# A second feed-forward's gate and up products: one group of seven over 1024 rows in place of two over 512

## The chip, the core and the metric

The kernel runs on one core of a Trainium2 chip. The core has five engines, each with its own instruction queue: TensorE multiplies, VectorE and ScalarE work element by element, GpSimd and SyncE are used here almost only to issue transfers. SBUF is the working memory with 128 partitions; PSUM holds TensorE's results, in eight banks of 128 x 512 float32 values.

The metric is the device time of one execution, in microseconds. The kernel before takes 1819.21 us (median of three runs, 1818.37 to 1819.67).

## What is computed

The reference is one layer of a streaming encoder on 256 rows of 2048 values: a half feed-forward, a mixer (a state-space group and an attention group between an input and an output projection), a second half feed-forward, and a gated embedding. The change touches the second feed-forward alone:

```python
def swiglu(h, w_gate, w_up, w_down):
    return (jax.nn.silu(h @ w_gate) * (h @ w_up)) @ w_down

x = x + 0.5 * swiglu(rms_norm(x, ffn2_norm[i]), ffn2_w_gate[i], ffn2_w_up[i], ffn2_w_down[i])
```

`h` is 256 x 2048, `w_gate` and `w_up` are 2048 x 5632, `w_down` is 5632 x 2048, all in float32.

## The kernel before

**Precision.** Every float32 operand is split into a high part (`hi`, a cast on ScalarE) and a low part (`lo`, a subtraction on VectorE; both in `split`, lines 178 to 187). A product is three matmuls: high by high, low by high, high by low. One matmul takes 128 rows of the contraction, 128 tokens and 512 columns.

**Blocks.** Gate and up are computed in 11 blocks of 512 columns (`f` = 0 to 10, the loop in `ffn`, line 633), gate and up of a block together. The 2048 rows of the contraction are four quarters of 512 (`kb` = 0 to 3); a quarter of one weight for one block is a load of 1 MB, into one of five `raw` buffers. A quarter is two halves; a half (128 x 1024 values) is split into a pair `hi`, `lo`. Pairs come from seven buffers in turn (`weight_pair`, line 288: four `whi`/`wlo`, three `shi`/`slo`; before the first chunk only the four).

**Columns.** `Seven.column` (line 591) multiplies a quarter in the plain way: per half 12 matmuls, 6 for each of the two token tiles.

**Chunks: seven products in place of eight.** `Seven.chunk` (line 566) treats a quarter of both weights as a 2 x 2 by 2 x 2 block product by the scheme of Strassen and Winograd: left blocks are two halves of the contraction by two token tiles, right blocks are `b11`, `b21` (gate) and `b12`, `b22` (up). It takes seven products of 6 matmuls, 42 in place of 48. For that VectorE forms three sums of weights (`t1`, `t2`, `t4`), GpSimd adds a fourth by an accumulating transfer (`b12 += b22`), and the sums of activations are formed once, by `whole_rows` and `sum_forms`. The products go into seven PSUM banks (1 to 7, and 8 for columns); `opened`, `gated` and `ended` (lines 647 to 688) put them together: one ScalarE copy, four 512-wide and two 1024-wide additions on VectorE, two SiLU on ScalarE, and the multiplication of gate and up. `turned` then transposes the block on VectorE, and SyncE moves its quarters into place (`turn_quarters`).

**The second feed-forward.** Block 0 multiplies quarter 1 by columns, quarter 0 by a chunk, quarters 2 and 3 by columns, and forms the activation sums of quarters 0 and 1 on the way. Blocks 1 to 10 each do: chunk of quarter 0, gate columns of quarters 2 and 3, chunk of quarter 1, up columns of quarters 2 and 3.

**What sets the order.** Each engine's instructions run in one fixed order that is planned when the kernel is built. TensorE's and SyncE's are close to the order of the code; VectorE's and ScalarE's are mixed from several products. An instruction waits for the data and the buffers it needs. `put_off(n, ...)` places work n steps later; a step is two products in a chunk or one column half.

Of the kernel before, what the change touches and what calls it, by code (L numbers as in the profile page):

```python
# [9 lines left out]
F32 = mybir.dt.float32  # L10
# [23 lines left out]
def layer_kernel(ctx: ExitStack, tc: tile.TileContext, a: dict, shapes: dict, out: bass.AP):  # L34
# [38 lines left out]
    def phase(name):  # L73
        return tc.tile_pool(name=name, bufs=1, reuse_waits="tile")
# [103 lines left out]
    def split(hi, lo, src, scale=None, pinned=False):  # L178

        if scale is None:  # L180
            copy = nc.scalar.copy(hi, src)  # L181
            if pinned:
                pin(copy)
            rest = nc.vector.tensor_tensor(out=lo, in0=src, in1=hi.bitcast(F32), op=ALU.subtract)  # L184
# [130 lines left out]
        nc.sync.dma_start(raw[:, :nk, :], quarter(w, k0 // 4, n0))  # L315
        return weight_split(raw, nk, own)

    def gemm_half(ps, half, ts, start, stop, cols=slice(0, NB)):

        (ahi, alo), (h, hi, lo) = half  # L320
        for j in range(2):
            for t in ts:
                lh = ahi[:, 2 * h + j, t * P : (t + 1) * P]
                ll = alo[:, 2 * h + j, t * P : (t + 1) * P]
                nc.tensor.matmul(ps[t], lhsT=lh, rhs=hi[:, j, cols], start=start and j == 0, stop=False)  # L325
                nc.tensor.matmul(ps[t], lhsT=ll, rhs=hi[:, j, cols], start=False, stop=False)  # L326
        for j in range(2):
            for t in ts:
                lh = ahi[:, 2 * h + j, t * P : (t + 1) * P]
                nc.tensor.matmul(ps[t], lhsT=lh, rhs=lo[:, j, cols], start=False, stop=stop and j == 1)  # L330

    def gemm_block(act, w, n0, nkt, first=()):

# [108 lines left out]
    def whole_rows(pool, parts, pinned=False):  # L442

        hi, lo = parts
        u = pool.tile([P, 2, NB], F32, tag="sum", name=uid("whole"), bufs=2)
        added = nc.vector.tensor_tensor(
            out=u.rearrange("p j n -> p (j n)"), in0=hi.bitcast(F32).rearrange("p j t -> p (j t)"),
            in1=lo.bitcast(F32).rearrange("p j t -> p (j t)"), op=ALU.add,
        )
# [4 lines left out]
    def sum_forms(pool, u, kind="n"):  # L454
# [4 lines left out]
        for z, (x, y, op) in enumerate((  # L459
            (a21, a22, ALU.subtract), (s[:, 0], a11, ALU.subtract),  # L460
            (a11, a21, ALU.subtract), (a12, s[:, 1], ALU.add),
        )):
            nc.vector.tensor_tensor(out=s[:, z], in0=x, in1=y, op=op)
        both = halves(kind)
        split(*both, sums.rearrange("p j n -> p (j n)").rearrange("p (z t) -> p z t", z=4))
        return both

# [135 lines left out]

    shared = (1, 5, 6, 7)

    def ffn(i, xn, nxt, bg=None):
        wg, wu, wd = (a[f"ffn{i}_w_{s}"] for s in ("gate", "up", "down"))
        hT = []
# [7 lines left out]
        turns = sevens  # L616
        sums = []
        mids = {}

        def turned(hp, f, hh):  # L620
            pair, n_pair = f // 2, min(2, NF - f // 2 * 2) * 4
# [11 lines left out]
        for f in range(NF):  # L633
            for kb, (at, steps) in enumerate(((2, 8), (5, 11))):
                if bg and f == at:
                    put_off(steps, lambda kb: sums.append(sum_forms(sevens, whole_rows(sevens, xn(kb), pinned=True), "h")), kb)
            if prep and f == early:
                finish(prep)
                side.close()
                prep = None  # L640
                turns = pools.enter_context(phase(f"turns{i}"))
                hp = pools.enter_context(phase(f"h{i}b"))
            if f >= early or f in alone:
                sg, hh = com("sg"), com("h")
                gate_cols, up_cols = ([u[:, t * NB : (t + 1) * NB] for t in range(TT)] for u in (sg, hh))

                def opened(s, g=gate_cols, u=up_cols):
                    nc.scalar.copy(g[0], s.bank(1))
                    nc.vector.tensor_tensor(out=u[0], in0=s.bank(6), in1=g[0], op=ALU.add)
                    nc.vector.tensor_tensor(out=u[1], in0=s.bank(7), in1=u[0], op=ALU.add)  # L650

                def gated(s, g=gate_cols, u=up_cols, hh=hh):
                    for z, (ps, other) in enumerate(((s.bank(2), g[0]), (s.bank(4), u[1]))):
                        nc.vector.tensor_tensor(out=g[z], in0=ps, in1=other, op=ALU.add)
                        nc.scalar.activation(g[z], g[z], AF.Silu, scale=xn.rs(z))
# [5 lines left out]
                s = Seven(xn, lambda kb: sums[kb], ((wg, f * NB), (wu, f * NB)), sevens, turns)  # L661
                if f == 0:
                    sums.append(sum_forms(sevens, whole_rows(sevens, xn(0))))
                    s.column(0, (1,))
                    s.column(1, (1,))
                    s.chunk(0, shared)
                    put_off(0, opened, s)
                    s.column(0, (2,))
                    s.column(1, (2,))
                    s.column(0, (3,), True)  # L670
                    sums.append(sum_forms(sevens, whole_rows(sevens, xn(1))))
                elif f in alone:
                    s.single(0, gate_cols[0], *up_cols)
                    s.column(0, (1, 2, 3), True)
                else:
                    s.chunk(0)
                    s.column(0, (2, 3))
                    s.chunk(1, (*shared, 2, 4))
                    put_off(0, opened, s)
                put_off(0, gated, s)  # L680

                def ended(s, g=gate_cols, u=up_cols, hh=hh, f=f, hp=hp):
                    nc.vector.tensor_tensor(out=hh, in0=s.banks[3.8], in1=hh, op=ALU.add)
                    for t in range(TT):
                        nc.vector.scalar_tensor_tensor(
                            out=u[t], in0=u[t], scalar=xn.rs(t), in1=g[t], op0=ALU.mult, op1=ALU.mult
                        )
# [36 lines left out]
            put_off(2, turned, hp, f, hh)  # L724
# [1074 lines left out]
```

## Time and profile before

| | |
|---|---|
| median of three runs | 1819.21 us |
| the profiled execution, its own time | 1818.46 us |
| its span, first to last instruction | 1816.4 us |
| mean granted TensorE clock | 0.999 |
| second feed-forward, gate and up (blocks 0 to 10) | about 1028 to 1480 us of the span |

The profile is one execution, taken by the hardware profiler. Its page gives the busy time of each engine: PE is TensorE, DVE is VectorE, ACT is ScalarE, POOL is GpSimd, SP is SyncE. Its views used below are the waits (which engine waited for which, us in total, how often, the longest), the busy time in stretches, the groups of like instructions (line, engine, operation, output<-input, shapes, count; busy us, mean ns of one; idle time before them and what ended it), the timeline (start, duration, engine, line, operation) and the issues of transfers (KB each, median us to landing). An instruction's duration in the timeline overlaps the next one's, so that the spacing of starts says what one costs.

### The profile page before, as it was taken

Reading aid. Unit: us, or ns where it says so; the run is one execution under the profiler, and the core shown is the slowest. Engines: PE = TensorE matmul, PEld = TensorE weight load, DVE = VectorE, ACT = ScalarE, POOL = GpSimd, SP = SyncE. Lnnn points to the kernel's source line nnn. Section 1 sums busy time; section 2 is a strip of 40 time slices with the busy share of each in tenths; the row PEclk is TensorE's granted clock in tenths of the full one; section 3 lists DMA queues with packets and bytes.
Section 4 is the critical chain, followed back from the end, with each engine's and each line's share of the span. In section 5 each row is a group of like instructions: output and inputs, shape, how many; then the busy total and the mean of one; then the engine's idle time right before and its main releaser. Section 6 shows DMA issues by size and latency. Waiting matters only on the chain.

```text
span 1816.4 us, 24219 instructions
## 1 busy us (share of the span) xinstructions
PE 1806.7 (99%) x8918; PEld 1496.6 (82%) x8918; DVE 1573.9 (87%) x1839; ACT 1065.3 (59%) x1240; POOL 106.2 (6%) x162
## 2 busy tenths in 40 slices
PE   9999999999999999999999999999999999999998
PEld 7888888888888888888898888888888888888887
DVE  8978889999998896697567899999999999889775
ACT  7445455656565665455695566555565566567664
POOL 0020100000000001110021000000000010000000
PEclk9999999999999999999999999999999999999999
DMA  8799867777776667674636787787767787666563
GB/s 321 268 292 301 269 221 232 235 259 228 262 261 226 190 226 262 188 255 163 218 139 215 234 297 225 263 268 235 232 231 236 241 277 242 220 209 228 195 243 128
DMA packets 107655, 428.41 MB, mean 236 GB/s; under 512 B 24368, under 2 KB 48336, under 8 KB 65136
## 3 DMA queue, kind: packets, MB, share of 16 engines
q1 hardware_dynamic: 96256, 390.06, 60.8%
q0 software_dynamic: 10560, 35.40, 9.0%
q8 instruction: 70, 1.15, 0.2%
q10 hardware_dynamic: 720, 1.41, 0.2%
q14 instruction: 49, 0.40, 0.1%
HBM read 372.41 MB, written 10.88 MB: 211 GB/s over the span
## 4 chain that ended last, share of the span: by engine, by line
PE 96%; DVE 1%; DMA 1%; issue 1%; ACT 1%; SPq 0%; DVEq 0%; ACTq 0%
PE acc L325 16%; PE acc L326 16%; PE acc L330 16%; PE aux L330 7%; PE aux L326 7%; PE aux L325 7%; PE acc L509 5%; PE acc L506 5%; PE acc L507 5%; PE aux L509 3%; PE aux L506 3%; PE aux L507 3%; DMA raw<-in_ffn_w_gate 0%; PE aux L1210 0%; PE acc L1466 0%
## 5 line engine op out<-in xcount | busy, mean ns | idle before, releaser
L184 DVE TENSOR_TENSOR wlo<-raw,whi 128x1024 fp32r<-128x1024 f32 x480 | 580.7, 1222 | 123.5 <-ACT whi L181 120.5
L181 ACT CAST whi<-raw 128x1024 fp32r<-128x1024 f32 x480 | 498.2, 1050 | 291.9 <-PE acc L326 181.8
L325 PE MATMUL acc<-whi,nhi 128*128 128x512 f32 x908 | 356.3, 392 | 2.8 <-ACT whi L277 2.3
L326 PE MATMUL acc<-whi,nlo 128*128 128x512 f32 x908 | 353.7, 390 | 0.0
L330 PE MATMUL acc<-wlo,nhi 128*128 128x512 f32 x908 | 252.5, 389 | 0.0
L184 DVE TENSOR_TENSOR slo<-raw,shi 128x1024 fp32r<-128x1024 f32 x186 | 226.1, 1216 | 15.8 <-ACT shi L181 15.5
L181 ACT CAST shi<-raw 128x1024 fp32r<-128x1024 f32 x186 | 195.2, 1049 | 62.1 <-DMA raw<-in_ffn_w_down 20.3
L325 PEld LDWEIGHTS acc<-whi,nhi 128*128 128x128 f32 x908 | 170.4, 188 | 40.3 <-ACT whi L277 3.5
L330 PEld LDWEIGHTS acc<-wlo,nhi 128*128 128x128 f32 x908 | 170.3, 188 | 35.9 <-DVE wlo L184 0.3
L326 PEld LDWEIGHTS acc<-whi,nlo 128*128 128x128 f32 x908 | 170.5, 188 | 34.8 <-DVE nlo L278 0.3
L181 ACT CAST whi<-sum 128x1024 fp32r<-128x1024 f32 x79 | 83.3, 1054 | 159.6 <-DVE sum L513 141.5
L181 ACT CAST shi<-sum 128x1024 fp32r<-128x1024 f32 x59 | 62.1, 1053 | 104.0 <-DVE sum L513 90.8
L513 DVE TENSOR_TENSOR sum<-sum,raw 128x1024 f32<-128x1024 f32 x92 | 112.1, 1219 | 1.0
L184 DVE TENSOR_TENSOR wlo<-sum,whi 128x1024 fp32r<-128x1024 f32 x79 | 96.2, 1220 | 7.3 <-ACT whi L181 6.7
L574 POOL DMA_DIRECT2D raw<-raw x44 | 38.2, 867 | 1035.7 <-DVE sum L513 595.0
L325 PE MATMUL aux<-whi,nhi 128*128 128x512 f32 x220 | 85.6, 389 | 0.0
L326 PE MATMUL aux<-whi,nlo 128*128 128x512 f32 x220 | 85.6, 389 | 0.0
L184 DVE TENSOR_TENSOR slo<-sum,shi 128x1024 fp32r<-128x1024 f32 x59 | 72.0, 1220 | 1.2 <-ACT shi L181 0.5
L330 PE MATMUL aux<-wlo,nhi 128*128 128x512 f32 x220 | 67.7, 389 | 0.0
L325 PE MATMUL acc<-whi,hhi 128*128 128x512 f32 x156 | 60.7, 389 | 0.0
L326 PE MATMUL acc<-whi,hlo 128*128 128x512 f32 x156 | 60.7, 389 | 0.0
L513 DVE TENSOR_TENSOR sum<-raw,raw 128x1024 f32<-128x1024 f32 x46 | 56.0, 1217 | 5.1 <-DMA raw<-in_ffn_w_down 4.2
(390 smaller groups left out, 3404.1 us busy)
## 6 DMA issues: line engine op xcount, KB each, us to landing
raw<-in_ffn_w_up SPq DMA_DIRECT2D x88, 1024.0 KB, 5.8
raw<-in_ffn_w_down SPq DMA_DIRECT2D x88, 1024.0 KB, 4.9
raw<-in_ffn_w_gate SPq DMA_DIRECT2D x86, 1024.0 KB, 6.9
raw<-in_w_in SPq DMA_DIRECT2D x32, 1024.0 KB, 5.5
raw<-raw POOLq DMA_DIRECT2D x46, 512.0 KB, 5.6
raw<-in_w_out SPq DMA_DIRECT2D x16, 1024.0 KB, 4.9
raw<-in_w_ple_gate SPq DMA_DIRECT2D x16, 1024.0 KB, 5.5
hT<-mid SPq DMA_DIRECT2D x160, 64.0 KB, 4.8
```

What stands on the lines that cost most here:

```text
L181: copy = nc.scalar.copy(hi, src)
L184: rest = nc.vector.tensor_tensor(out=lo, in0=src, in1=hi.bitcast(F32), op=ALU.subtract)
L325: nc.tensor.matmul(ps[t], lhsT=lh, rhs=hi[:, j, cols], start=start and j == 0, stop=False)
L326: nc.tensor.matmul(ps[t], lhsT=ll, rhs=hi[:, j, cols], start=False, stop=False)
L330: nc.tensor.matmul(ps[t], lhsT=lh, rhs=lo[:, j, cols], start=False, stop=stop and j == 1)
L506: nc.tensor.matmul(ps, lhsT=lh[j], rhs=hi[:, j], start=begin and j == 0, stop=False)
L507: nc.tensor.matmul(ps, lhsT=ll[j], rhs=hi[:, j], start=False, stop=False)
L509: nc.tensor.matmul(ps, lhsT=lh[j], rhs=lo[:, j], start=False, stop=z in final and j == 1)
L513: nc.vector.tensor_tensor(out=t, in0=x, in1=y, op=ALU.add)
L574: nc.gpsimd.dma_start(b12, b22, accum_op=ALU.add)
```

## The change

Blocks 1 to 10 of the second feed-forward no longer use two chunks of 512 rows. A new class `Wide` does one group of seven over 1024 rows: quarter 0 of gate and up are `b11` and `b12`, quarter 1 are `b21` and `b22`, and each of the seven products now has 12 matmuls (two halves). The running sums that `opened` and `gated` formed on VectorE stay in PSUM: between products ScalarE copies one bank into another with the sign turned (`handed`), and the next product is added on top of it. A block so needs five banks; `b5` is copied out once by ScalarE.

In five blocks (2, 4, 6, 8, 9) a third group, of quarter 2, is joined: each of the seven products gets one more half (18 matmuls), and the columns are then only those of quarter 3. The other five blocks keep columns of quarters 2 and 3, after the seven products.

Block 0 is reordered: columns of quarters 0 and 1, a chunk of quarter 2 (with sign-turned sums, kept in buffers of their own, `third`), then the activation forms of quarters 0 and 1 together (`wide_forms`), then columns of quarter 3. The first feed-forward is unchanged.

The core of the diff:

```diff
+    def wide_forms(pool, parts, kind="n"):
+
+        u0, u1 = (whole_rows(pool, p) for p in parts)
+        (a11, a21), (a12, a22) = ([u[:, :, 4 * t : 4 * t + 4] for t in range(TT)] for u in (u0, u1))
+        for o, x, y in ((a22, a21, a22), (a21, a11, a21), (a11, a11, a22), (a12, a12, a11)):
+            nc.vector.tensor_tensor(out=o, in0=x, in1=y, op=ALU.subtract)
+        forms = []
+        for u in (u0, u1):
+            both = halves(kind)
+            split(*(in_32(v) for v in both), u)
+            forms.append(both)
+        return forms
...
+        def multiply(self, ps, z, parts, fresh=False):
+            left = self.left(z)
+            for i, ((lh, ll), (hi, lo)) in enumerate(zip(left, parts)):
+                for j in range(2):
+                    nc.tensor.matmul(
+                        ps, lhsT=lh[j], rhs=hi[:, j], start=fresh and i == 0 and j == 0, stop=False,
+                        skip_group_check=True,
+                    )
+                    nc.tensor.matmul(ps, lhsT=ll[j], rhs=hi[:, j], start=False, stop=False, skip_group_check=True)
+                for j in range(2):
+                    nc.tensor.matmul(
+                        ps, lhsT=lh[j], rhs=lo[:, j], start=False, stop=i == len(left) - 1 and j == 1,
+                        skip_group_check=True,
+                    )
+            step()
+
+        def handed(self, out, ps):
+            nc.scalar.activation(out, ps, AF.Copy, scale=-1.0)
+
+        def seven(self):
+
+            if ring[0] is None:
+                ring[:] = [self.turns, 0]
+            b11, b12 = self.load(0, 0), self.load(1, 0)
+            if self.third:
+                ga, ua_ = self.load(0, 2), self.load(1, 2)
+                b11, b12 = b11 + ga[:1], b12 + ua_[:1]
+            b22, b21 = self.load(1, 1), self.load(0, 1)
+            t = [self.pool.tile([P, 2, NB], F32, tag="sum", name=uid("sum"), bufs=2) for _ in range(2)]
+            if self.third:
+                b22, b21 = b22 + ua_[1:], b21 + ga[1:]
+                t.append(self.third[1].tile([P, 2, NB], F32, tag="sum3", name=uid("sum3")))
+
+            def add(x, y):
+                for o, u, v in zip(t, x, y):
+                    nc.vector.tensor_tensor(out=o, in0=u, in1=v, op=ALU.add)
+
+            b2, b5 = acc(), acc()
+            p = self.prepare(b11)
+            self.multiply(b2, "11", p, True)
+            add(b11, b12)
+            for u, v in zip(b12, b22):
+                nc.gpsimd.dma_start(u, v, accum_op=ALU.add)
+            p = self.prepare(t)
+            self.multiply(b5, 0, p, True)
+            double = aux()
+            b3, b8 = double[:, :NB], double[:, NB:]
+            add(t, b22)
+            p = self.prepare(t)
+            self.handed(b3, b2)
+            self.multiply(b3, 1, p)
+            p = self.prepare(b21)
+            self.multiply(b2, "12", p)
+            b4 = acc()
+            p = self.prepare(b12)
+            self.handed(b4, b3)
+            self.multiply(b4, 2, p)
+            add(t, b21)
+            p = self.prepare(b22)
+            self.multiply(b3, 3, p)
+            p = self.prepare(t)
+            self.handed(b8, b4)
+            self.multiply(b4, "22", p)
...
+            if not bg and f:
+                joined = f in (2, 4, 6, 8, 9)
+                s = Wide(
+                    xn, sums, ((wg, f * NB), (wu, f * NB)), sevens, turns, (third, narrow) if joined else None
+                )
+                s.seven()
+                sg, hh, five = com("sg"), com("h"), com("sq")
+                put_off(0, nc.scalar.copy, five, s.five)
+                kbs = (3,) if joined else (2, 3)
+                s.column(0, kbs)
...
+                put_off(0, gate)
+                s.column(1, kbs)
+                nc.vector.tensor_tensor(
+                    out=hh.rearrange("p (t n) -> p t n", t=TT), in0=s.double.rearrange("p (t n) -> p t n", t=TT),
+                    in1=five.unsqueeze(1).to_broadcast([P, TT, NB]), op=ALU.add,
+                )
+                for t in range(TT):
+                    cols = slice(t * NB, (t + 1) * NB)
+                    nc.vector.scalar_tensor_tensor(
+                        out=hh[:, cols], in0=hh[:, cols], scalar=xn.rs(t), in1=sg[:, cols], op0=ALU.mult, op1=ALU.mult
+                    )
...
                 if f == 0:
-                    sums.append(sum_forms(sevens, whole_rows(sevens, xn(0))))
+                    s.column(0, (0,))
+                    s.column(1, (0,))
                     s.column(0, (1,))
+                    sum_forms(sevens, whole_rows(sevens, xn(2)), both=third, turned=True)
                     s.column(1, (1,))
-                    s.chunk(0, shared)
+                    s.chunk(2, shared)
                     put_off(0, opened, s)
-                    s.column(0, (2,))
-                    s.column(1, (2,))
+                    sums = wide_forms(sevens, [xn(0), xn(1)])
                     s.column(0, (3,), True)
-                    sums.append(sum_forms(sevens, whole_rows(sevens, xn(1))))
```

`prepare` loads nothing: it splits the two or three halves that it is given into pairs. A step is now one product of the seven, or one column half.

More of the change, by code (lines that the diff above doesn't have):

```diff
@@ L316, in weight_halves, with gemm_half @@
         return weight_split(raw, nk, own)
-    def gemm_half(ps, half, ts, start, stop, cols=slice(0, NB)):
+    def gemm_half(ps, half, ts, start, stop, cols=slice(0, NB), joined=False):
         (ahi, alo), (h, hi, lo) = half
@@ L324, in gemm_half @@
                 ll = alo[:, 2 * h + j, t * P : (t + 1) * P]
-                nc.tensor.matmul(ps[t], lhsT=lh, rhs=hi[:, j, cols], start=start and j == 0, stop=False)
-                nc.tensor.matmul(ps[t], lhsT=ll, rhs=hi[:, j, cols], start=False, stop=False)
+                nc.tensor.matmul(
+                    ps[t], lhsT=lh, rhs=hi[:, j, cols], start=start and j == 0, stop=False, skip_group_check=joined
+                )
+                nc.tensor.matmul(
+                    ps[t], lhsT=ll, rhs=hi[:, j, cols], start=False, stop=False, skip_group_check=joined
+                )
         for j in range(2):
@@ L329, in gemm_half @@
                 lh = ahi[:, 2 * h + j, t * P : (t + 1) * P]
-                nc.tensor.matmul(ps[t], lhsT=lh, rhs=lo[:, j, cols], start=False, stop=stop and j == 1)
+                nc.tensor.matmul(
+                    ps[t], lhsT=lh, rhs=lo[:, j, cols], start=False, stop=stop and j == 1, skip_group_check=joined
+                )
     def gemm_block(act, w, n0, nkt, first=()):
@@ L452, in whole_rows, with sum_forms @@
         return u.rearrange("p j n -> p (j n)").rearrange("p (j x b) -> p j x b", j=4, b=32)
-    def sum_forms(pool, u, kind="n"):
+    def sum_forms(pool, u, kind="n", both=None, turned=False):
         sums = pool.tile([P, 2, NB], F32, tag="sum", name=uid("rows"), bufs=2)
@@ L618, in ffn @@
         mids = {}
+        if not bg:
+            side = pools.enter_context(ExitStack())
+            narrow = side.enter_context(phase(f"third{i}"))
+            third = [narrow.tile([P, 4, T], F32R, name=uid("third")) for _ in range(2)]
         def turned(hp, f, hh):
@@ L648, in opened @@
                     nc.scalar.copy(g[0], s.bank(1))
-                    nc.vector.tensor_tensor(out=u[0], in0=s.bank(6), in1=g[0], op=ALU.add)
+                    nc.vector.tensor_tensor(
+                        out=u[0], in0=g[0], in1=s.bank(6), op=ALU.add if bg else ALU.subtract
+                    )
                     nc.vector.tensor_tensor(out=u[1], in0=s.bank(7), in1=u[0], op=ALU.add)
```

63 lines of the change are left out of this document (59 added, 4 removed).

## The prediction

> **What bounds the kernel now.** I read the page first, then TensorE's waits and the busy time by block in the stage that is changed, and then the timelines of TensorE, VectorE and SyncE there. The page's first lines:
>
> ```profile
> span 1816.4 us, 24219 instructions
> PE 1806.7 (99%) x8918; PEld 1496.6 (82%) x8918; DVE 1573.9 (87%) x1839; ACT 1065.3 (59%) x1240; POOL 106.2 (6%) x162
> ```
>
> TensorE looks full. Whether it is bound by itself is read from its waits between 940 and 1500 us, of which there is one, and from the blocks (columns: stretch, length, then busy us of PE, PEld, DVE, ACT, POOL with their instructions, clock, DMA share, GB/s):
>
> ```profile
> PE acc L509 <- DVE slo L184: 0.4, 1, 0.4
> ```
>
> ```profile
> 1030.00:1071.90 41.90, 41.46 (x183) 34.02 (x182) 41.67 (x56) 27.39 (x35) 2.30 (x3) 1.00 0.79 277
> 1071.90:1112.70 40.80, 40.80 (x182) 33.78 (x181) 40.06 (x40) 25.15 (x28) 1.74 (x2) 1.00 0.70 232
> 1112.70:1153.50 40.80, 40.80 (x182) 33.78 (x181) 38.54 (x38) 22.20 (x24) 1.71 (x2) 1.00 0.79 258
> ...
> 1439.40:1480.60 41.20, 41.20 (x183) 34.12 (x182) 40.13 (x43) 25.12 (x27) 5.28 (x9) 1.00 0.84 272
> ```
>
> The rows are blocks f=0, 1, 2 and 10. Three rows of TensorE's timeline give the price of a matmul: f=0 starts, its chunk starts 48 matmuls later, f=1 starts.
>
> ```profile
> 1027.96 0.39 PE L325 MATMUL acc<-whi,hhi 128*128 128x512 f32 x1
> ...
> 1038.85 0.39 PE L506 MATMUL acc<-whi,hhi 128*128 128x512 f32 x1
> ...
> 1070.86 0.39 PE L506 MATMUL acc<-shi,hhi 128*128 128x512 f32 x1
> ```
>
> 10.89 us / 48 = 0.2269 us a matmul. A block after f=0 has 180 (two chunks of 42, eight column halves of 12): 40.84 us, the length of its row. So TensorE sets the pace, with nothing between matmuls; f=0 has 186, 42.2 us, and took 42.9. But VectorE is busy for 38.5 to 41.7 us of the same rows: it is the engine that is late next. Its real price is the spacing of starts (VectorE's timeline, block f=10):
>
> ```profile
> 1431.15 0.68 DVE L654 TENSOR_TENSOR sg<-acc,sg 128x512 f32<-128x512 f32 x1
> 1431.75 0.68 DVE L654 TENSOR_TENSOR sg<-acc,h 128x512 f32<-128x512 f32 x1
> ...
> 1441.65 1.41 DVE L685 SCALAR_TENSOR_TENSOR h<-h,sm,sg 128x512 f32<-128x512 f32 x2
> 1442.97 1.30 DVE L217 STREAM_TRANSPOSE mid<-h 128x512 f32<-128x512 f32 x2
> 1444.19 1.18 DVE L184 TENSOR_TENSOR wlo<-raw,whi 128x1024 fp32r<-128x1024 f32 x1
> ...
> 1446.43 1.22 DVE L184 TENSOR_TENSOR wlo<-raw,whi 128x1024 fp32r<-128x1024 f32 x1
> ...
> 1457.78 1.22 DVE L184 TENSOR_TENSOR wlo<-raw,whi 128x1024 fp32r<-128x1024 f32 x1
> ```
>
> Between the last two are nine more of the same width: 11.35 us for ten, 1.135 each ("a wide op" below). A 512-wide one takes 0.60, the two gatings 1.32, the two transposes 1.22. A block before: 28 wide ops (14 splits and 6 sums in chunks, 8 column splits) 31.8; four 512-wide and one wide in opened and gated 3.5; wide, gatings, transposes at the end ("the tail") 3.7; together 39.0 of 40.8.
>
> **The change: what TensorE saves.** Two groups of seven over 512 rows are 84 matmuls, one group over 1024 rows is 84 too. Only the third group saves: 7 x 18 + 48 = 174 instead of 180, in five blocks: 30 matmuls, 6.8 us. That is the ceiling of the gain.
>
> **What VectorE does per block.** opened and gated go (-3.5), the tail stays. A block without the third group ("plain"): 28 wide + 3.7 = 35.5 of 40.8. One with it ("joined"): 21 + 4 splits, 9 sums, 34 wide = 38.6 + 3.7 = 42.3 against TensorE's 39.5. A pair: 77.8 against 80.3. The average fits, but only with work done ahead.
>
> **How far ahead it must be.** The seven products come first now, P1 to P7, and the column halves, cheap for VectorE (1.135 per 2.72 us of TensorE), last. In a plain block the first half of P6 is VectorE's 17th wide op: 19.3 us, with the last block's tail 23.0. TensorE gets there after 5 x 2.72 = 13.6 us and wants the low part 4 matmuls (0.9) later. So VectorE must stand 8.5 us ahead when P1 starts. Joined: 25th op, 28.4 + 3.7 - 5 x 4.08 - 0.9 = 10.8. The seven pairs of split buffers allow, at P1, six pairs and the sums between: 10 ops (11.4 us) in a plain block, 12 (13.6) in a joined one. Enough, where the block before had plain columns (21.8 us of TensorE for 9.1). A joined block uses up 34.1 + 3.7 - 28.6 = 9.2 of it, and its columns return 10.9 - 4.5 = 6.4: f=8 starts with 13.6, f=9 with 10.8 against a need of 10.8, f=10 with 8.0 against 8.5. Cost there: 0.5 us (0 to 3, since a lost DMA or cast shows at once).
>
> **What f=0 does to that lead.** Here I choose the sign. VectorE from f=0's start to f=1's:
>
> ```profile
> 1027.27 1.22 DVE L184 TENSOR_TENSOR wlo<-raw,whi 128x1024 fp32r<-128x1024 f32 x1 [3.13 <-ACT whi L181]
> ...
> 1030.94 1.18 DVE L184 TENSOR_TENSOR wlo<-raw,whi 128x1024 fp32r<-128x1024 f32 x1
> ...
> 1034.30 1.21 DVE L513 TENSOR_TENSOR sum<-raw,raw 128x1024 f32<-128x1024 f32 x1
> ...
> 1042.25 1.22 DVE L446 TENSOR_TENSOR whole<-hhi,hlo 128x1024 f32<-128x1024 f32 x1
> ...
> 1053.17 1.27 DVE L194 SCALAR_TENSOR_TENSOR nlo<-h,gains,nhi 128x256 fp32r<-128x256 f32 x3
> 1054.35 1.22 DVE L184 TENSOR_TENSOR wlo<-raw,whi 128x1024 fp32r<-128x1024 f32 x1
> ...
> 1060.24 1.22 DVE L184 TENSOR_TENSOR slo<-raw,shi 128x1024 fp32r<-128x1024 f32 x1
> ```
>
> ```profile
> DVE wlo L184 <- ACT whi L181: 3.1, 1, 3.1
> ```
>
> The second view is VectorE's waits of 1028 to 1075 us: one, and that before 1030.94. 1034.30 is the chunk's first sum; 1060.24 is already f=1's first split, 10.6 us before P1. The change puts four column pairs ahead of the chunk and the wide forms behind it: two whole rows, four 512-wide differences, two splits, 2.3 + 2.4 + 2.3 = 7.0 us, in place of the forms of quarter 1. They can't move up: their two buffers are those of the chunk's sums. And the chunk can't move up either, because of SyncE's queue and the landing (behind it: ScalarE's wait for the load of 1040.15, and two rows of the DMA issues of 1005 to 1075 us, with KB and median us to landing):
>
> ```profile
> 1024.16 0.33 SPq L520 DMA_DIRECT2D raw<-in_ffn_w_up  x1
> 1031.05 8.55 SPq L230 DMA_DIRECT2D h<-mid  x12
> 1040.15 0.34 SPq L315 DMA_DIRECT2D raw<-in_ffn_w_gate  x1
> 1040.54 2.52 SPq L230 DMA_DIRECT2D h<-mid  x4
> ```
>
> ```profile
> 1045.73 1.05 ACT L181 CAST whi<-raw 128x1024 fp32r<-128x1024 f32 x1 [1.55 <-DMA raw<-in_ffn_w_gate]
> ```
>
> ```profile
> raw<-in_ffn_w_up SPq DMA_DIRECT2D x6, 1024.0 KB, 6.9
> raw<-raw POOLq DMA_DIRECT2D x2, 512.0 KB, 5.2
> ```
>
> The queue keeps the order of the code. Today the chunk's loads (until 1024.16) are ahead of the twelve quarter moves, which wait until 1031.05 for the last x block; after the change the up load of quarter 1 stands behind four, the chunk's two loads behind twelve. So they go out near 1040, the gate lands near 1045.7, the up near 1047. VectorE, from 1030.94, has until then five column splits, the forms of quarter 2 (about 4), four 256-wide of 0.39 and small ones (about 1): 12.3 us, so it is free at 1043.2 and then idle. The first sum moves from 1034.3 to 1047 (bounds: 1043.2, if the loads came earlier, and 1049, if the load took 2 us longer).
>
> Then in a row: the chunk's other 9 wide ops 10.2, parts of quarter 3 1.6, opened 1.2, wide forms 7.0, four column splits 4.5, gated 2.3: 26.8, and f=1 up to P6 23.0. P6's low part is there at 1096.8. TensorE, unhindered, wants it at 1027.96 + 42.2 + 13.6 + 0.9 = 1084.7. **f=1 is 12.1 us late** (8.3 to 14.1 by the bounds). From then on f=1's columns restore the lead, as above.
>
> The gap would open at P2, which needs the first sum of f=1 and so the forms: 5 to 9 us without a matmul, where the windows above show clock 1.00 throughout. The Trainium skill (TensorE: Matmul & The Clock Gate, "HAM oscillation") says that a gap over about 3.4 us halves TensorE's clock. No run here shows such a gap; by the rule P3 to P5 would be slower, but P6 is the later one by 2 us or more, so the sum would rise by 0 to 2 us.
>
> **What costs nothing.** ScalarE's rows:
>
> ```profile
> L181 ACT CAST whi<-raw 128x1024 fp32r<-128x1024 f32 x131 | 135.5, 1048 | 47.8 <-PE acc L326 25.6 <-DMA raw<-in_ffn_w_up 5.2 <-DMA raw<-in_ffn_w_down 4.0
> L655 ACT ACTIVATE sg<-sg,sm 128x512 f32<-128x512 f32 x22 | 14.7, 717 | 26.6 <-DVE sg L654 26.6
> L648 ACT COPY sg<-acc 128x512 f32<-128x512 f32 x11 | 6.3, 576 | 0.7 <-PE acc L509 0.7
> ```
>
> Three PSUM copies more per block at 0.58 (the nearest row is L648, which writes SBUF; at most L655's 0.72, at least nothing), three casts more in a joined block: at most 25 x 1.05 + 4 x 0.58 + 2 x 0.72 = 30 of 39.5 us. Each copy has one whole product (2.7 or 4.1 us) between its source's end and its reader. Uncovered, it would cost 0.6 to 1.6 (a cast in front). Loads stay eight per block. GpSimd's accumulating moves become three instead of two in a joined block; from the sum that frees their target to the split that reads it are 12 wide ops, 13.6 us, against 5.2 to land (8 ops, 9.1 us, in a plain block). Each of the five raw buffers is now reloaded some seven wide ops (7.9 us) before use, against 6.9 to land: hidden, and if a load takes longer, the excess is lost only where the lead is short (in the 0 to 3 above).
>
> **Rivals.** *A, forecast:* -6.8 + 12.1 + 0.5 and f=0's 0.7 won back: +5.1 on 1818.46, 1823.6; on the median of 1819.21, which is 0.75 higher, 1824.3. Own range 1820 (8.3 for 12.1, no 0.5) to 1829 (14.1, and 3 for 0.5). *B, not slower:* VectorE gets into f=1 with 8.5 us in hand after all, if the chunk and the forms fill its idle time before 1047. For it: VectorE doesn't keep the order of the code (the whole rows at 1042.25 stand in the code behind column halves that ran later), and it has 3.13 us idle at 1027. Against it: the two buffers and SyncE's queue, which keeps its order. Then TensorE pays only matmuls: 1812.4. It decides at P6 of f=1: ready by 1084.7 or not. *C:* the tail of f=0 (3.7) is put behind P6 and the loads are early: 4.6 to 8.3 us late, 1816.3 to 1820. *D, slower by another way:* the copies wait for TensorE at the head of ScalarE's queue, with the casts of the next products behind them; if a copy is queued one product early, casts start up to 2.7 us later, and where VectorE has no slack (five joined blocks) 1 to 2 us each are lost: 5 to 10 on top of B, 1817 to 1822, or on top of A, up to 1834. Against it: ScalarE has some 9 us to spare in a block, and each copy stands behind casts of a later product only if the order was planned wrongly. The Trainium skill (PSUM — Partial Sum Buffer, "Engine vs sequencer instructions") says that ScalarE's queue is strictly first in, first out; that lets D happen, it has no price, and no run here shows such a copy.
>
> **How the numbers follow.** Measurement can tell 0.2%, 3.6 us: 1815.6 to 1822.8. A 0.55 (0.08 of it under 1822.8), B 0.25, C 0.13, D 0.07 (on A). Faster 0.25, same 0.21, slower 0.54. Leaving out B would leave out more than 2 in 10, so the range runs from 1812 to A's 1829.
>
> **What would show it.** Right: TensorE waits for VectorE's low parts and sums within f=1 only, f=1 lasts about 52 us, the blocks 2, 4, 6 and 8 about 39.5, the others 40.8. Wrong: f=1 at 41 with 1812 (B); waits of TensorE on ScalarE's copies (D); joined blocks over 40.8, then VectorE's ledger is mis-sized.

## The result, and the profile after

| | before | after |
| --- | --- | --- |
| median of six runs beside each other (us) | 1818.43 | 1832.68 |
| lowest to highest (us) | 1817.99 to 1819.67 | 1830.53 to 1834.74 |
| profiled execution: time, span (us) | 1818.46, 1816.4 | 1834.74, 1833.0 |

The ratio is 1.0078, 95% interval 1.0065 to 1.0091: 14.2 us slower, where +5.1 was forecast. The profiled execution after lies 2.1 us above its median.

The page's first lines after:

```profile
span 1833.0 us, 24280 instructions
PE 1810.9 (99%) x8888; PEld 1494.3 (82%) x8888; DVE 1576.0 (86%) x1821; ACT 1099.5 (60%) x1286; POOL 110.6 (6%) x167
```

The 30 matmuls are gone (8918 to 8888), and TensorE still counts as 99% busy: these two lines alone would hide the loss. TensorE's waits between 940 and 1500 us (total, times, longest), where before had one row of 0.4:

```profile
PE acc L666 <- ACT whi L181: 2.0, 1, 2.0
PE aux L334 <- DVE wlo L184: 1.9, 1, 1.9
PE aux L672 <- DVE wlo L184: 1.8, 1, 1.8
PE aux L666 <- ACT shi L181: 1.6, 1, 1.6
PE acc L666 <- ACT aux L679: 1.3, 5, 0.3
...
```

Busy time by stretch (columns as in the prediction): f=0 and f=1 together, f=2 to 7, f=8, f=9, f=10.

```profile
1028.66:1128.39 99.73, 90.75 (x367) 71.21 (x366) 92.36 (x104) 57.77 (x71) 6.34 (x8) 0.93 0.71 236
1128.39:1371.19 242.80, 241.99 (x1063) 198.68 (x1062) 235.74 (x217) 163.84 (x178) 13.18 (x15) 1.00 0.78 253
1371.19:1411.19 40.00, 39.73 (x175) 32.59 (x174) 40.00 (x38) 29.08 (x32) 2.14 (x3) 1.00 0.73 244
1411.19:1453.24 42.05, 40.18 (x176) 32.43 (x174) 39.72 (x38) 26.14 (x29) 2.24 (x3) 1.00 0.73 232
1453.24:1495.20 41.96, 40.86 (x180) 33.41 (x179) 39.23 (x39) 29.52 (x33) 4.37 (x8) 1.00 0.83 274
```

The ten rows of this view add up to 12.9 us, less than was lost: a lowered clock and the restart after a wait stand in no row. So the loss is read from lengths: the length of a row against its matmuls at 0.2269 us. f=0 and f=1: 99.7 for 366 matmuls (83.0), 16.7 lost, where before lost 0.7. f=2 to 7: 242.8 for 1062 (241.0), 1.8 lost, 0.6 a pair. f=8 to 10, to the first matmul of the down stage at 1495.50 (0.3 us behind the last row's end): 124.3 for 528 (119.8), 4.5 lost. So -6.8 + 16.0 + 1.8 + 4.5 = +15.5 (16.0 is 16.7 less the 0.7 of before); f=0 also starts 0.7 later than before, and the two profiled executions differ by 16.3. VectorE is busy for 235.74 of 242.80 us in f=2 to 7, 97%.

VectorE's timeline in f=0 and f=1:

```profile
1048.38 1.22 DVE L519 TENSOR_TENSOR sum<-raw,raw 128x1024 f32<-128x1024 f32 x1 [1.05 <-DMA raw<-in_ffn_w_up]
...
1061.11 1.22 DVE L184 TENSOR_TENSOR wlo<-raw,whi 128x1024 fp32r<-128x1024 f32 x1 [1.84 <-ACT whi L181]
1062.25 2.35 DVE L452 TENSOR_TENSOR whole<-hhi,hlo 128x1024 f32<-128x1024 f32 x2
...
1080.68 1.22 DVE L697 TENSOR_TENSOR sum<-raw,raw 128x1024 f32<-128x1024 f32 x1
...
1090.92 1.23 DVE L184 TENSOR_TENSOR slo<-sum,shi 128x1024 fp32r<-128x1024 f32 x1 [0.81 <-ACT shi L181]
...
1100.02 1.22 DVE L184 TENSOR_TENSOR wlo<-raw,whi 128x1024 fp32r<-128x1024 f32 x1
```

The chunk's first sum starts at 1048.38 (forecast 1047), the wide forms at 1062.25, f=1's first sum at 1080.68, and P6's first split at 1100.02: its low part is there at 1101.2, where 1096.8 was forecast. VectorE stands still only twice between, for 1.84 and 0.81 us. Without these stops its operations from the first sum to P6's low part take 50.2 us, and 49.8 were forecast.

TensorE shows no wait at P6 itself. It waits for the products before, and so comes late to P6 (its timeline: the first matmuls of P2 and of P3, and the one that takes P6's low part):

```profile
1083.09 0.50 PE L666 MATMUL acc<-whi,nhi 128*128 128x512 f32 x1 [2.03 <-ACT whi L181]
...
1090.95 0.79 PE L666 MATMUL aux<-shi,nhi 128*128 128x512 f32 x1 [1.62 <-ACT shi L181]
...
1102.03 0.61 PE L672 MATMUL aux<-wlo,nhi 128*128 128x512 f32 x2
```

The low part is taken 0.8 us after it is there, so VectorE's row sets this point within 0.8 us. TensorE waits in f=0 too: 1.1 and 1.0 us in the chunk's products, 1.9 in the last columns.

VectorE's stop of 1.84 us begins with GpSimd's accumulating transfer for the chunk (GpSimd's timeline, then ScalarE's):

```profile
1050.30 0.89 POOL L580 DMA_DIRECT2D raw<-raw  x1 [18.62 <-DMA raw<-in_ffn_w_gate]
```

```profile
1060.03 1.99 ACT L181 CAST whi<-raw 128x1024 fp32r<-128x1024 f32 x2 [3.33 <-DMA raw<-raw]
```

Issued at 1050.30, it lets ScalarE's cast start at 1060.03: 9.7 us, not the 5.2 of the forecast's row. In the seven runs below that keep this chunk it took 9.7 to 10.8 us, so it is no accident of one execution. The chunk's transfer before took 4.9 us, while the DMA moved 147 GB/s; here it moves 351. That this is the reason isn't shown. SyncE's timeline for the loads of the forecast:

```profile
1024.85 0.33 SPq L315 DMA_DIRECT2D raw<-in_ffn_w_up  x1
1031.95 7.63 SPq L230 DMA_DIRECT2D h<-mid  x12
1040.14 0.34 SPq L526 DMA_DIRECT2D raw<-in_ffn_w_gate  x1
1040.58 0.37 SPq L526 DMA_DIRECT2D raw<-in_ffn_w_up  x1
```

The chunk's two loads do stand behind the twelve quarter moves; the up load of quarter 1 doesn't (1024.85).

In f=1 the granted clock falls (the number behind POOL's):

```profile
1070.00:1080.00 10.00, 8.07 (x29) 6.13 (x29) 10.00 (x11) 4.03 (x5) 0.00 (x0) 0.83 0.44 170
1080.00:1090.00 10.00, 6.43 (x17) 3.80 (x15) 10.00 (x11) 3.31 (x5) 1.74 (x2) 0.68 0.64 142
1090.00:1100.00 10.00, 9.05 (x34) 7.28 (x35) 9.19 (x9) 9.06 (x10) 0.00 (x0) 0.80 0.44 97
```

### The profile page after: what moved, and what is told of

Read it like the earlier page. It is cut to its first block, busy times and chain, and to the rows that moved or that the text cites. A ratio compares the mean times of both kernels' runs of the same rounds, so it can differ in the third digit from the quotient of the medians.

```text
span 1833.0 us, 24280 instructions
## 1 busy us (share of the span) xinstructions
PE 1810.9 (99%) x8888; PEld 1494.3 (82%) x8888; DVE 1576.0 (86%) x1821; ACT 1099.5 (60%) x1286; POOL 110.6 (6%) x167
## 5 line engine op out<-in xcount | busy, mean ns | idle before, releaser
L325 PE MATMUL acc<-whi,nhi 128*128 128x512 f32 x884 | 347.3, 393 | 2.0 <-ACT whi L277 1.9
L328 PE MATMUL acc<-whi,nlo 128*128 128x512 f32 x884 | 344.8, 390 | 0.0
L334 PE MATMUL acc<-wlo,nhi 128*128 128x512 f32 x884 | 245.7, 390 | 0.2 <-DVE wlo L184 0.2
L181 ACT CAST whi<-sum 128x1024 fp32r<-128x1024 f32 x90 | 94.8, 1053 | 124.7 <-DVE sum L519 61.2
L184 DVE TENSOR_TENSOR wlo<-sum,whi 128x1024 fp32r<-128x1024 f32 x90 | 109.4, 1220 | 9.0 <-ACT whi L181 8.3
L328 PE MATMUL aux<-whi,nlo 128*128 128x512 f32 x192 | 75.2, 391 | 0.0
L325 PE MATMUL aux<-whi,nhi 128*128 128x512 f32 x192 | 75.1, 391 | 0.0
L519 DVE TENSOR_TENSOR sum<-sum,raw 128x1024 f32<-128x1024 f32 x52 | 63.5, 1221 | 0.9
L334 PE MATMUL aux<-wlo,nhi 128*128 128x512 f32 x192 | 59.7, 392 | 1.9 <-DVE wlo L184 1.9
L580 POOL DMA_DIRECT2D raw<-raw x24 | 20.8, 866 | 653.6 <-DVE sum L519 321.9
L697 DVE TENSOR_TENSOR sum<-sum,raw 128x1024 f32<-128x1024 f32 x50 | 59.6, 1220 | 0.5
```

The lines of the kernel that those rows point to most:

```text
L519: nc.vector.tensor_tensor(out=t, in0=x, in1=y, op=ALU.add)
L580: nc.gpsimd.dma_start(b12, b22, accum_op=ALU.add)
L697: nc.vector.tensor_tensor(out=o, in0=u, in1=v, op=ALU.add)
```

## The experiments

The theory: VectorE's work of f=0 (chunk, wide forms, column splits) starts late and runs in a row, and f=1 waits for it. Rivals: the lower clock, the joined blocks, the handed copies, the late moves. Times are medians; ratios are to the kernel before on the same chip. Blocks are dated by VectorE's closing operation of a block (L799), which starts at 1128.95 for f=1 in the changed kernel.

### The wide forms left out

```diff
-                    sums = wide_forms(sevens, [xn(0), xn(1)])
+                    sums = [xn(0), xn(1)]
```

> Leaves out the 7.0 us of VectorE work (and two casts) that form the activation differences of quarters 0 and 1; the seven products of blocks 1 to 10 read the plain parts instead. Theory 1 (block 1 is late because VectorE enters it in debt): the loss of blocks 0 and 1, 16 us in the changed kernel, shrinks by 7 us and by most of the 5 to 6 us that the lowered clock costs: ratio to the kernel before about 1.001 to 1.003 instead of 1.0078, block 1's gaps nearly gone, clock 1.00 there. Theory 2 (the copies at the head of ScalarE's queue, or the transfers, hold block 1 up): within 2 us of the changed kernel, gaps stay.

1824.24 us, ratio 1.0029 [1.0019, 1.0039]. VectorE's timeline at the end of f=1:

```profile
1121.26 1.22 DVE L799 TENSOR_TENSOR h<-aux,sq 128x1024 f32<-128x1024 f32 x1
```

7.7 us earlier, for 7.0 us of VectorE work taken out, and 8.4 us less in all: what VectorE has to do in f=0 stands on the path nearly one to one. Other than expected, waits of 1.7, 0.7 and 1.6 us stay, and the clock still falls to 0.83, from 1080 to 1090 us.

### Block 0 by columns alone, and the forms later

```diff
+            if not bg and f == 0:
+                s = Seven(xn, None, ((wg, 0), (wu, 0)), sevens, turns)
+                sg, hh = com("sg"), com("h")
+                for kb in range(2):
+                    s.column(0, (kb,))
+                    s.column(1, (kb,))
+                sums = wide_forms(sevens, [xn(0), xn(1)])
+                s.column(0, (2,))
+                s.column(1, (2,))
+                s.column(0, (3,), True)
...
                 s.seven()
+                if f == 1:
+                    sum_forms(sevens, whole_rows(sevens, xn(2)), both=third, turned=True)
```

> Block 0 is multiplied by columns alone (192 matmuls for 186), its two 1024-row forms stand right behind the columns of quarter 1, and the forms of quarter 2 move into block 1. Theory 1: VectorE has 9 wide operations less behind the late chunk loads, enters block 1 ahead, no gap and no lowered clock in blocks 0 and 1: 16 us less 1.4 us, so about 1818 us, ratio 0.999 to 1.001. Theory 2: block 1 still loses 5 us or more, since its own copies, sums and transfers are unchanged: ratio over 1.003.

1818.20 us, ratio 0.9995 [0.9986, 1.0005]; f=1 ends at 1113.25, 15.7 us earlier, TensorE has no wait in f=0 and f=1, and the clock is 1.00 throughout. As far as is known, this run leaves the values that `handed` copies into `double` out of block 1's sums, after narrow matmuls had written its banks last. The next one writes both banks full width first, and has them in:

```diff
+                spare = aux()
+                for k in range(2):
+                    nc.tensor.matmul(
+                        spare[:, k * NB : (k + 1) * NB], lhsT=xn(0)[0][:, k, :P], rhs=xn(0)[0][:, 2 * k : 2 * k + 2], start=True, stop=True
+                    )
```

> Block 0 of the second gate/up by columns only: 192 matmuls in place of 186, no chunk sums, no P of its own; the wide forms are made during its second half, the third forms in block 1; two full-width matmuls first write both banks of the pair that block 1 uses next. Theory (VectorE's debt of sums, forms and splits in block 0 makes block 1 late): blocks 0 and 1 lose under 1 us, block 1's closing operation L799 starts at 1113 to 1114, where the changed kernel has 1128.95; +1.4 us for the six matmuls, +0.5 for the two; the whole at 1818 to 1820. Rival (the lateness comes with the wide forms' own dependencies, whenever they are made): L799 at 1121 or later, the whole at 1825 or more.

1820.01 us (1818.78 to 1822.83), ratio 1.0007 [0.9998, 1.0017]. Its windows, f=0 with f=1, then f=2 to 10, and its one row of TensorE's waits from 1020 to 1500 us:

```profile
1029.28:1114.62 85.34, 85.07 (x375) 70.12 (x374) 75.14 (x85) 53.98 (x67) 5.48 (x7) 1.00 0.77 266
1114.62:1479.78 365.16, 362.98 (x1592) 297.44 (x1591) 355.27 (x330) 249.13 (x271) 21.91 (x28) 1.00 0.79 255
```

```profile
PE acc L666 <- ACT aux L679: 2.3, 7, 0.6
```

VectorE has 75 us of work in f=0 and f=1 instead of 92, and the loss falls from 16.7 to 0.5 us (85.34 for 374 matmuls, 84.86). f=1 ends at 1115.87 (L801 in this kernel), 13.1 us earlier: about 2 later than expected, far from the rival's 1121. The debt is shown, by e1_no_forms in part and here nearly whole. This run takes out the chunk, its late loads and its transfer together; how much each weighs is read from the trace alone. What is left is in the second row: 1590 matmuls are 360.8 us, and 4.4 are lost, about half of it in the only wait that remains, for ScalarE's handed copy, and the rest mostly in the restarts after it (last section). That is the other half of the answer: f=2 to 10 gain 2.1 us on before (367.2), not 6.8, and block 0 costs 1.8 more for its eight extra matmuls. In its profiled execution the rest comes behind the stage, among it a wait that neither before nor after has (TensorE's timeline):

```profile
1733.62 0.50 PE L325 MATMUL acc<-whi,nhi 128*128 128x512 f32 x1 [1.53 <-ACT whi L181]
```

### The gaps filled with matmuls

```diff
             self.multiply(b2, "11", p, True)
+            self.keep(p)
...
             self.multiply(b5, 0, p, True)
+            self.keep(p)
...
+                for hi, lo in parts:
+                    for i in range(6):
+                        nc.tensor.matmul(
+                            self.idle, lhsT=lh[:, 0, :P], rhs=hi[:, i % 2], start=True, stop=True,
```

In block 1 alone: 24 matmuls behind P1 and P2, whose result isn't read.

> 24 further matmuls into an unused PSUM bank, placed by the plan into the gaps of products 1 to 3 of block 1; nothing else changes. If the lowered clock (matmuls at 0.425 us instead of 0.227 between 1073 and 1094 us) costs time of its own, keeping TensorE busy holds the clock at 1.00 after 1081 us and saves 2 to 5 us: ratio 1.005 to 1.0065. If VectorE alone sets the end of block 1, the time is unchanged or up to 2 us longer.

1833.39 us, ratio 1.0077 [1.0062, 1.0092]. Its windows, then P6's first split and the end of f=1 (L815 is the L799 of this kernel) in VectorE's timeline:

```profile
1070.00:1080.00 10.00, 8.08 (x36) 6.36 (x35) 10.00 (x11) 3.77 (x5) 0.00 (x0) 1.00 0.45 163
1080.00:1090.00 10.00, 7.98 (x34) 5.63 (x32) 9.89 (x12) 4.29 (x6) 1.74 (x2) 1.00 0.67 147
1090.00:1100.00 10.00, 7.64 (x29) 5.81 (x30) 9.02 (x8) 8.01 (x9) 0.00 (x0) 0.93 0.40 84
```

```profile
1100.11 1.22 DVE L184 TENSOR_TENSOR wlo<-raw,whi 128x1024 fp32r<-128x1024 f32 x1
...
1130.85 1.22 DVE L815 TENSOR_TENSOR h<-aux,sq 128x1024 f32<-128x1024 f32 x1
```

The clock is 1.00 where it was 0.83 and 0.68, and VectorE starts P6's first split at the same time as in the changed kernel (1100.11 and 1100.02). f=1 ends 1.9 us later, not earlier, but the run isn't a clean test of that end: it has 24 matmuls more and a new wait for a handed copy (2.4 us at 1098.15), behind which the clock falls again. What the lower clock can have cost the changed kernel is bounded by its own trace: the 0.8 us by which TensorE takes P6's low part late, and the 0.81 us that VectorE stands after the clock has fallen, together 1.6. The lower clock is a sign of the waits more than their price.

### Fewer joined blocks

```diff
-                joined = f in (2, 4, 6, 8, 9)
+                joined = False
```

> No block is joined: 30 matmuls come back (6.8 us) and 30 VectorE operations go. Theory 1 says that blocks 0 and 1 are as before this edit (16 us lost) and that the joined blocks gave back about 6 of their 6.8 us (0.6 us in each pair, 3.6 us in blocks 9 and 10): the time stays within 2 us of the changed kernel, ratio 1.007 to 1.009. Rival: the third group is what breaks VectorE's budget, then the time falls by 5 us or more.

1838.53 us, ratio 1.0108 [1.0093, 1.0123]: 5.9 us over the changed kernel, so the joined blocks give nearly what their 30 matmuls are worth. Neither of the two expectations came. f=0 and f=1 together take 100.4 us (1029.20 to 1129.57) without any joined block, 99.7 with them; they aren't the cause. With `joined = f in (2, 4, 6, 8)`:

> The changed kernel with four joined blocks (2, 4, 6, 8) in place of five: block 9 is plain with 15 steps, 180 matmuls instead of 174. Theory (two joined blocks after one another, with 11 steps each, bring the late quarter moves and accumulating transfers of blocks 8 to 10, some 3.6 us): +1.4 us for six matmuls, -2.6 in block 9 and -1 in block 10: the whole at 1829.5 to 1831.5. Rival (the loss at the end comes with block 10 whatever stands before it): the whole at 1833.5 to 1834.5.

1831.93 us, ratio 1.0071 [1.0056, 1.0086], between the two expectations. Block 9's wait is gone, but its six matmuls are back: the fifth joined block is worth nothing that can be told.

### The late moves, and a repeat

```diff
-                turn_quarters(hf, mids[pair], 8)
+                turn_quarters(hf, mids[pair], 4)
```

> The changed kernel with the quarter moves of hT put off by 4 steps instead of 8 after a pair's transposes. Theory (the moves of a pair hold its mid buffer until the next pair's transposes have to write it; in blocks 8 and 9 with 11 steps each they come too late): VectorE's 2.2 us wait at L217 in block 9 goes, block 9 shortens from 42.05 to 40.0 us or less, and the whole goes from 1832.7 to 1829.5 to 1831. Rival (block 9 is late because of the accumulating transfers, which land late under load): L217's wait goes but block 9 stays above 41.5 and the time within 0.7 us. Second rival: SyncE, which is in order, now stands at the quarter moves until the transposes are done and the weight loads behind them come late: slower by 1 to 4 us.

1839.30 us, ratio 1.0114 [1.0098, 1.0131], 6.6 us slower than the changed kernel. Two windows of it, f=2 and f=3, and a row of the DMA queue's waits in this pair of blocks:

```profile
1128.29:1168.29 40.00, 39.73 (x176) 32.58 (x174) 37.48 (x35) 26.76 (x29) 1.77 (x2) 1.00 0.71 239
1168.29:1210.69 42.40, 41.39 (x182) 33.63 (x180) 41.19 (x38) 27.60 (x31) 2.65 (x3) 1.00 0.81 259
```

```profile
SPq L315 <- DMA raw<-raw: 13.1, 1, 13.1
```

VectorE's wait at L217 is gone, but f=9 is longer, 43.0 us, and VectorE waits 10.5 us in f=2 to 10 for ScalarE's `whi`, where it waited 2.2. f=2 is as long as in the changed kernel (40.0), f=3 takes 42.40 where it took 40.9. SyncE's load stands 13.1 us for an accumulating transfer to release its buffer, where the same row of the changed kernel has 4.1; GpSimd issued that transfer at 1163.77 instead of 1161.71. So the moves aren't free where they are, but earlier they cost more. How their place sets the transfer's stays open.

```diff
-            p = self.prepare(t)
             self.handed(b8, b4)
+            p = self.prepare(t)
```

> The changed kernel with the third handed copy (b4 to b8) put ahead of the casts of the last operand, not behind them. Theory (the copy stands behind casts that wait for a weight buffer, and TensorE's last product waits for the copy, 0.27 us and a restart of 0.3 in each joined block, 0.7 in some): blocks 2 to 7 lose about 0.2 us a pair instead of 0.6, the wait of L666 on ScalarE's L679 goes from 1.3 us in 5 to under 0.3, the whole at 1830.5 to 1832. Rival (a copy that waits at the head of ScalarE's queue holds back the casts behind it): the waits of TensorE on ScalarE's casts whi and shi grow by 0.5 to 1 us a block, the whole at 1834 to 1840.

1833.84 us (1831.65 to 1835.50), ratio 1.0081. ScalarE and VectorE got the order that they had in the changed kernel, so this run says nothing of the copy; it is a second look at the same order. TensorE's timeline, the first matmuls of f=8, 9 and 10:

```profile
1371.52 0.39 PE L666 MATMUL acc<-whi,hhi 128*128 128x512 f32 x1
...
1411.55 0.39 PE L666 MATMUL acc<-shi,hhi 128*128 128x512 f32 x1
...
1451.76 0.39 PE L666 MATMUL acc<-whi,hhi 128*128 128x512 f32 x1
```

f=9 lasts 40.2 us here, not 42.05, and the wait of 1.8 us on `wlo`, at f=9's P6, isn't there. Nor is a stop of VectorE that stands before it in the changed kernel's profile (VectorE's timeline, the transposes of f=8, which wait for a quarter move):

```profile
1422.15 1.30 DVE L217 STREAM_TRANSPOSE mid<-h 128x512 f32<-128x512 f32 x2 [2.20 <-DMA hT<-mid]
```

In f=8 to 10 this execution loses 2.3 us where the other lost 4.5. That term varies from one execution to the next.

### The handed copy held ahead of the casts

```diff
-            nc.scalar.activation(out, ps, AF.Copy, scale=-1.0)
+            return nc.scalar.activation(out, ps, AF.Copy, scale=-1.0)
...
-            p = self.prepare(t)
-            self.handed(b8, b4)
+            with tc.issue_after(self.handed(b8, b4).ins):
+                p = self.prepare(t)
```

> The changed kernel with the third handed copy (b4 to b8) really ahead of the casts of the last operand on ScalarE: the casts are queued behind it. Theory (the copy is ready 4 us before TensorE needs it, and only the casts ahead of it, which wait for weight buffers, make it late): the waits of L666 on ScalarE's L679 (1.1 to 1.3 us in four or five joined blocks) go, and with each the slower restart after it: 0.3 to 0.6 us in each of five joined blocks, 1.5 to 3 us less than the changed kernel: 1829.7 to 1831.2. Rival (the copy at the head of ScalarE's queue waits for the product before it, and the casts behind it come late): TensorE's waits on the casts of L181 grow, the whole at 1833 to 1838.

1868.38 us, ratio 1.0265 [1.0251, 1.0279]: 36 us slower than the changed kernel (34 by the ratios). ScalarE's timeline in f=2, then TensorE's: the first matmul of P6, the last two and the first of P7:

```profile
1143.89 1.06 ACT L181 CAST shi<-raw 128x1024 fp32r<-128x1024 f32 x1 [0.20 <-PE acc L670]
1153.86 0.58 ACT L679 ACTIVATE aux<-acc 128x512 f32<-128x512 f32 x1 [8.92 <-PE aux L672]
```

```profile
1149.59 0.39 PE L666 MATMUL aux<-whi,nhi 128*128 128x512 f32 x1
...
1153.21 0.61 PE L672 MATMUL aux<-slo,third 128*128 128x512 f32 x2
1155.45 0.50 PE L666 MATMUL acc<-whi,hhi 128*128 128x512 f32 x1 [1.62 <-ACT whi L181]
```

The copy stands 8.92 us at the head of ScalarE's queue, with P7's casts behind it, and starts 0.2 us after P6 ended (1153.66 by the spacing of starts), not after P5 (1149.6), whose sum it copies. Each of the ten blocks has such a hold, of 5.3 to 9.0 us. This is the forecast's rival D, at several times its price. With block 0 by columns too:

> Block 0 by columns, as in e6_plain_open, together with the handed copy kept ahead as in e13_copy_kept. Theory (the two losses are separate and add up): 1.5 to 3 us under e6_plain_open's 1820.0, that is 1817 to 1818.5, under the kernel before by 0.7 to 2 us. Rival (the blocks behind are at VectorE's limit, so that what TensorE no longer waits for the copy it waits for VectorE's splits): 1819.5 to 1821.

> As e12_open_copy, with four joined blocks (block 9 plain) in place of five. Theory (without block 0's debt the last joined block pays its six matmuls): slower than e12_open_copy by 1 to 1.4 us. Rival (two joined blocks after one another bring late moves and waits): faster than e12_open_copy by 0.5 to 2 us.

1856.91 us, ratio 1.0204 [1.0190, 1.0218], and 1853.56, 1.0182 [1.0167, 1.0198]: the casts behind the copy set the time again, and what the two expectations set apart can't be read. Why the copy waits for P6 is asked by writing it ahead of P6, with no hold on ScalarE's order:

```diff
+            self.handed(b8, b4)
             self.multiply(b3, 3, p)
             p = self.prepare(t)
-            self.handed(b8, b4)
```

> Block 0 by columns, as in e6_plain_open, with the third handed copy (b4 to b8) written ahead of the product P6 into b3 and not behind it; where ScalarE issues it is left to the planner. b3 and b8 are the two halves of one PSUM tile. Theory (the copy is bound to P6 by their common tile, not by its data: behind P6 it waited for P6's end, ahead of P6 it starts 0.2 us after P5's end and P6 waits for it): P6 stands 0.5 to 1 us in those blocks where no column product is put between, P7's waits on L679 go; the whole at 1820 to 1827, and no ScalarE wait as long as the 8.9 us of e13_copy_kept. Rival (halves are tracked apart): P6 doesn't wait, P7's waits go too, 2 us under e6_plain_open: 1817 to 1818.5.

1822.72 us, ratio 1.0025 [1.0016, 1.0034], 2.7 us over e6_plain_open. The copy in f=3 in ScalarE's timeline, P6's first matmul in TensorE's, and the first row of TensorE's waits:

```profile
1169.01 0.58 ACT L679 ACTIVATE aux<-acc 128x512 f32<-128x512 f32 x1
```

```profile
1169.64 0.50 PE L666 MATMUL aux<-shi,nhi 128*128 128x512 f32 x1 [0.56 <-ACT aux L679]
```

```profile
PE aux L666 <- ACT aux L679: 3.9, 5, 2.4
```

Now the copy runs ahead of P6, and P6 (`aux`, b3) starts right behind its end (1169.59), though they write different halves of `double`. So it is in f=3, 5, 7, 9 and 10; in f=2, 4, 6 and 8 column matmuls are put in front of P6, and wait 0.7 us for a cast. The two halves are one tile to whoever sets the waits: written behind P6 the copy waits for P6, ahead of it P6 waits for the copy. In neither order is there a whole product to cover it.

No version beats the kernel before by what can be measured; e6_plain_open is 12.7 us faster than the changed one and level with before.

## Why the prediction was right and wrong

Between the forecast's +5.1 and the +16.2 of the two profiled executions lie 4.6 us in f=0 and f=1, 4.0 in f=8 to 10, 1.8 in f=2 to 7, and 0.7 by which f=0 starts later.

- **TensorE's saving, 6.8 us:** right (30 matmuls fewer, and e3_no_third loses 5.9 without them).
- **f=0 moves the lead, f=1 is late:** the mechanism was right, and the sign with it. Its size failed: 12.1 us was forecast, at most 14.1, and 16.7 were lost; the whole, 1832.7, is above A's 1829. The step that failed is "Then in a row ... 26.8, and f=1 up to P6 23.0": the operations were counted right (50.2 us for 49.8), but as if VectorE stood nowhere. It did for 1.84 us, since the accumulating transfer took 9.7 us where the row of before said 5.2, and for 0.81 in f=1. The bounds of this step held the load's lateness only, not a transfer inside the row. The first sum came 1.4 us later than 1047, half of it from f=0's later start, which isn't part of the loss. The last 0.8 is TensorE's, which takes P6's low part late and waits for P7's copy. The sign "within f=1 only" didn't hold, since TensorE waits in f=0 already. The remark on the up load of quarter 1 was wrong and changed nothing.
- **f=8 to 10, 0.5 (0 to 3):** mis-sized. They lost 4.5 us in one execution and 2.3 in the other. That leads of 10.8 against 10.8 were called enough was the weak point: in the first execution VectorE stood 2.2 us for a quarter move, and f=9's P6 came 1.8 late. The trace of e2_plain_block0 has the same pair, 1.3 and 1.3 us. The other large part is 1.1 us at a handed copy in f=10, which the forecast had at nothing.
- **"What costs nothing":** wrong for the copies. They cost up to 1.8 us in f=2 to 7 and most of the 4.4 in e6_plain_open. "Each copy has one whole product between its source's end and its reader" fails for the third, which shares its tile with that product's target.
- **Rival B** is the course that e6_plain_open takes in f=0 and f=1, and it doesn't come to 1812.4: copies and eight matmuls use up the gain. **Rival D** isn't what the changed kernel does, but e13_copy_kept shows it: 36 us, where 5 to 10 were priced. The Trainium skill (PSUM — Partial Sum Buffer, "Engine vs sequencer instructions") calls ScalarE's queue strict first in, first out; the 8.92 us with idle casts behind agree.
- **The clock:** the forecast gave it 0 to 2 us by the Trainium skill's rule (TensorE: Matmul & The Clock Gate, "HAM oscillation") of gaps over some 3.4 us. The clock did fall, to 0.68, after gaps of at most 2.03 us, so keeping each gap under the rule's length wasn't enough here. What it cost is at most about 1.6 us, an estimate from the changed kernel's trace (the section on the filled gaps). That P6 and not the slowed P3 to P5 would set the time was right, though not by the 2 us that were forecast.

## What to carry to other kernels

When work is moved to the second engine, ask for its lead at the first place that needs it, not for its share of a stage: TensorE, busy through the rest of the stage, can't win back what it waits in the first block, and whatever stands inside the debt (a transfer's landing too) is lost nearly one to one. Give an operation between two engines cover in the order that the waits are really set, by tile and not by the half that is touched. A copy that is moved up in an in-order queue, and has to wait there, holds up everything behind it.

## What the hardware showed besides

The granted clock fell to 0.68 in f=1 after several gaps of 0.9 to 2.0 us close together, while one gap of 1.76 us alone, in f=9 at 1434.83, left it at 1.00. A wait of TensorE costs more than its length (TensorE's timeline in f=2 of e8_copy_first):

```profile
1153.89 0.39 PE L328 MATMUL acc<-shi,nlo 128*128 128x512 f32 x1
1154.55 0.50 PE L666 MATMUL acc<-whi,hhi 128*128 128x512 f32 x1 [0.27 <-ACT aux L679]
1154.88 0.40 PE L670 MATMUL acc<-whi,hlo 128*128 128x512 f32 x1
```

From start to start 0.66 and 0.33 us instead of 0.2269 each: a wait shown as 0.27 takes 0.54.
